# Gates and gated unit by seven block products ahead of one mixing stage for both halves

## The chip, the cores and the metric

The kernel runs on one core of a Trainium2 chip. Its time is the device time of one execution in microseconds (us), 2001.92 as the median of three runs (2001.01 to 2002.47). The engines that matter are TensorE (PE in the profile; PEld is its loading of weights), VectorE (DVE), ScalarE (ACT), GpSimd (POOL) and SyncE (SP, here a queue of transfers). Each engine works off its own queue of instructions in order and waits, where it must, for the results of another engine or of a transfer.

## The reference

One layer of a language model's trunk, on x of 1024 tokens by 1024 channels, in float32. Cut to what matters:

```python
h = layer_norm(x, ln_in_g, ln_in_b)
u = h @ w_in                    # columns: a, g | z | x, B, C | dt | gate_a | gate_b
v = a * sigmoid(g)                              # gated unit, 1024 channels
v = silu(layer_norm(causal_dwconv(v, 31 taps))) # norm over channels, for each token
y_a = v @ w_conv_out
xbc = silu(causal_dwconv([x, B, C], 4 taps))
dt = softplus(dt_raw + dt_bias)
y = ssd_chunked(x, dt, -exp(a_log), B, C) + x * d_skip   # 32 heads in 4 groups, chunks of 128
y = rms_norm_by_group(y * silu(z)) * norm_w
y_b = y @ w_ssm_out                             # 2048 -> 1024
h = layer_norm(alpha * h + (sigmoid(gate_a) * y_a + sigmoid(gate_b) * y_b) @ w_o)
up = causal_dwconv(h @ w_ffn_up, 3 taps)        # 2 x 2816 channels
h = layer_norm(alpha * h + (silu(up[:2816]) * up[2816:]) @ w_ffn_down)
```

The scan `ssd_chunked` carries a state from chunk to chunk, so chunk c + 1 of a group needs the state that chunk c leaves.

## The kernel before

Tokens are worked on in two halves of 512 (HALF), channels in blocks of 128 (the partitions). Every operand of a large product is split into a high part (fp32r) and the rest, and a product of two is three matmuls, hi by hi, hi by lo, lo by hi (`mm3`). A weight tile of 128 x 1024 is loaded by SP, its high part is made by ACT, and its low part by DVE (`weights`). `project` multiplies such a tile with a split activation of eight slices, 24 matmuls of 128x512.

The program runs `ln_in_first` (norm of the first half, transposed to `hT0`), `mixers(0)`, `combine(0)` with the norm of the second half inside it, `out_proj`, `mixers(1)`, `combine(1)`, and the feed-forward part.

- `mixers(hh, hT)`: `first_columns` (dt, B, C of group 0), `time_steps` (softplus of dt and its running sums, a long chain of small steps in the tile `sp`), and then for each of four groups: columns B, C and four of x with their 4-tap convolution (`conv4`), the gate z, two channel blocks of the gated unit (`glu`, a weight for a and one for g), the scan of the group (`ssd_group`, four chunks), and the 31-tap convolution of the two blocks (`conv31`, on DVE, 30 instructions SCALAR_TENSOR_TENSOR for each block, "taps" below), at a low priority. At the end come the eight column blocks of gate_a.
- `combine(hh)`: the eight blocks of gate_b in turn with the second half of `w_ssm_out` (weights `sp`), the norm of the convolution over channels (the pieces `cc` come back from DRAM; POOL adds them up, TensorE averages over partitions with `mean_w`, DVE subtracts, ACT squares, POOL adds, and so on, until DVE and ACT write the split result `sT`), `w_conv_out` (weights `co`), and the split of the mixed result into `mixT`.
- The feed-forward up-projection already works with all 1024 tokens at once and with seven block products in place of eight (a 2 x 2 block product by Winograd's form of Strassen's method): `up_first` makes two of the seven and stores them to DRAM, `up_rest` the other five.

The order of the instructions on each engine is set when the kernel is built, by a scheduler which takes them in the order in which they are written, shifted by the numbers in `tc.high_priority(offset=...)`: a positive offset pulls a piece ahead, a negative one leaves it until nothing else is there.

The names of the profile: `sm` and `acc` are banks of PSUM, `w_xx` a split weight, `st_xx` its raw form, `c` and `v` the convolution's result and input, `stats` and `csq` the norm's sums. Lines that the prediction uses: L166 to L168 the three matmuls, L154 and L155 the split of a weight, L435 the taps, L493 the product `au` (on POOL) of the scan, L294 to L351 the time steps, L638 to L658 the norm, L182 and L183 the split of `sT`.

## Time and profile before

| what | value |
|---|---|
| median of three runs | 2001.92 us |
| profiled execution, its own time | 2004.89 us |
| its span | 2003.2 us |
| granted TensorE clock, mean | 0.997 |
| TensorE, DVE, ACT, POOL busy | 98%, 84%, 52%, 9% |

The same by stage (from the engines' busy times in stretches of the span, us):

| stage | from, to | TensorE | DVE | ACT | POOL |
|---|---|---|---|---|---|
| norm, first half | 0 to 41 | 25.9 | 28.3 | 14.0 | 10.9 |
| mixers, first half | 41 to 530 | 486.6 | 449.2 | 280.7 | 40.4 |
| combine and out-projection | 530 to 700 | 170.0 | 121.9 | 69.2 | 26.4 |
| mixers, second half | 700 to 1190 | 488.9 | 450.9 | 274.7 | 39.1 |
| combine, second half | 1190 to 1330 | 138.6 | 88.6 | 66.9 | 20.9 |
| up-projection | 1330 to 1770 | 439.8 | 357.9 | 237.9 | 39.9 |
| down-projection, last norm | 1770 to 2003 | 217.0 | 194.9 | 90.9 | 3.3 |

How to read the rows: a timeline row is start, duration, engine, line, operation, written tile, read tiles, shape and count, and in brackets how long the engine had been idle and for whom. A group's row has the busy time and the mean duration in ns of one instruction, and then the idle time before them. A waits row has the total, the number and the longest. Instructions overlap in their engine's pipeline, so the step from one start to the next is often shorter than a duration. A row of stretches has, after the bounds, the busy time of PE, PEld, DVE, ACT and POOL, the granted clock, the DMA share and GB/s.

### The profile page before, as it was taken

What the parts mean: (1) busy time and instruction counts of PE and PEld (TensorE: products, weight loads), DVE (VectorE), ACT (ScalarE), POOL (GpSimd) and SP (SyncE); (2) the same over time, 40 slices, a digit from 0 to 9 for tenths busy, and PEclk for the clock granted to TensorE, in tenths of its full rate; (3) what the DMA queues carried; (4) which work ended last, traced back from release to release, by engine and by line L of the source; (5) the groups of instructions that cost most, each with busy time, mean ns of one, the idle gap of its engine ahead of it and who ended that gap; (6) DMA issues with size and microseconds to landing.
All of it is one profiled execution on the core that took longest, in us unless ns stands there. A gap on an engine that the chain in (4) does not pass through costs nothing.

```text
span 2003.2 us, 24740 instructions
## 1 busy us (share of the span) xinstructions
PE 1966.7 (98%) x9092; PEld 1618.2 (81%) x9092; DVE 1691.6 (84%) x2243; ACT 1034.2 (52%) x1491; POOL 180.8 (9%) x189
## 2 busy tenths in 40 slices
...
PEclk9999999999999999999999999999999999999999
...
GB/s 211 95 74 95 79 78 118 95 110 101 165 207 163 164 121 74 85 90 85 116 90 111 100 170 124 132 283 236 144 183 181 182 173 190 165 278 299 197 244 126
DMA packets 109449, 297.12 MB, mean 148 GB/s; under 512 B 12560, under 2 KB 12560, under 8 KB 109328
## 3 DMA queue, kind: packets, MB, share of 16 engines
...
q8 instruction: 71, 1.16, 0.2%
...
## 4 chain that ended last, share of the span: by engine, by line
PE 71%; DVE 21%; DMA 4%; issue 3%; ACT 1%; DVEq 0%; SPq 0%; ACTq 0%
PE acc L168 16%; PE acc L167 16%; PE acc L166 16%; DVE c L435 8%; PE sm L168 6%; PE sm L167 6%; PE sm L166 6%; DMA do<-wdown 2%; DVE xbc L390 2%; PE sm L549 1%; PE sm L192 1%; DMA b_scr<-fo 1%; PE sm L530 1%; PE acc L372 1%; DVE w_so L155 1%
## 5 line engine op out<-in xcount | busy, mean ns | idle before, releaser
L435 DVE SCALAR_TENSOR_TENSOR c<-v,pc,c 128x512 f32<-128x512 f32 x480 | 375.4, 805 | 7.3 <-ACT c L424 5.9
L493 POOL TENSOR_TENSOR au<-seg_mv,head_of 128x1024 fp32r<-128x1024 f32 x32 | 76.8, 2399 | 908.3 <-PE sm L502 727.0
L166 PE MATMUL acc<-hT,w_c 128*128 128x512 f32 x376 | 150.3, 400 | 0.0
L167 PE MATMUL acc<-hT,w_c 128*128 128x512 f32 x376 | 149.9, 399 | 0.0
L168 PE MATMUL acc<-hT,w_c 128*128 128x512 f32 x376 | 147.7, 393 | 0.0
L1016 ACT CAST w_dn<-dr 128x1024 fp32r<-128x1024 f32 (+1 forms) x73 | 68.6, 944 | 82.3 <-DVE dr L953 30.8
L390 DVE SCALAR_TENSOR_TENSOR xbc<-u,pc,xbc 128x512 f32<-128x512 f32 x144 | 109.9, 775 | 0.8 <-ACT xbc L388 0.8
L167 PE MATMUL sm<-h1s,w_s 128*128 128x512 f32 x264 | 102.7, 389 | 0.0
L166 PE MATMUL sm<-h1s,w_s 128*128 128x512 f32 x264 | 102.7, 389 | 0.0
L168 PE MATMUL sm<-h1s,w_s 128*128 128x512 f32 x264 | 102.2, 389 | 0.0
L154 ACT CAST w_c<-st_c 128x1024 fp32r<-128x1024 f32 x50 | 52.6, 1051 | 94.2 <-PE acc L168 76.5
L167 PE MATMUL acc<-w_z,hT 128*128 128x512 f32 x256 | 100.9, 394 | 0.0
L166 PE MATMUL acc<-w_z,hT 128*128 128x512 f32 x256 | 100.8, 401 | 0.0
L168 PE MATMUL acc<-w_z,hT 128*128 128x512 f32 x256 | 100.4, 395 | 0.0
L167 PEld LDWEIGHTS acc<-hT,w_c 128*128 128x128 f32 x376 | 70.6, 188 | 17.8 <-issue 3.9
L168 PEld LDWEIGHTS acc<-hT,w_c 128*128 128x128 f32 x376 | 70.6, 188 | 17.0 <-issue 2.6
L166 PEld LDWEIGHTS acc<-hT,w_c 128*128 128x128 f32 x376 | 70.6, 188 | 16.9 <-issue 2.6
L1017 DVE TENSOR_TENSOR w_dn<-dr,w_dn 128x1024 fp32r<-128x1024 f32 (+1 forms) x73 | 78.5, 1087 | 3.2 <-ACT w_dn L1016 3.2
L155 DVE TENSOR_TENSOR w_c<-st_c,w_c 128x1024 fp32r<-128x1024 f32 x47 | 60.5, 1288 | 22.7 <-ACT w_c L154 22.7
L168 PE MATMUL acc<-h1b,w_ue 128*128 128x512 f32 x176 | 68.7, 394 | 0.0
L166 PE MATMUL acc<-h1b,w_ue 128*128 128x512 f32 x176 | 68.7, 390 | 0.0
L167 PE MATMUL acc<-h1b,w_ue 128*128 128x512 f32 x176 | 68.5, 389 | 0.0
...
## 6 DMA issues: line engine op xcount, KB each, us to landing
...
```

What stands on the lines that cost most here:

```text
L154: A.copy(w[:, 0, :], st)
L155: (eng or V).tensor_tensor(out=w[:, 1, :], in0=st, in1=w[:, 0, :].bitcast(F32), op=ALU.subtract)
L166: TE.matmul(ps, wa(0), xa(0), start=start, stop=False, skip_group_check=more)
L167: TE.matmul(ps, wa(0), xa(1), start=False, stop=False, skip_group_check=more)
L168: TE.matmul(ps, wa(1), xa(0), start=False, stop=stop, skip_group_check=more)
L192: TE.transpose(pt[:, i * P : (i + 1) * P], src[:, (q + i) * P : (q + i + 1) * P], ident)
L372: TE.matmul(ps[:, ts], w[:, i, k * P : (k + 1) * P], hT[:, j, k, ts], start=n == 0 and k == 0, stop=n == 2 and k == KD - 1,)
L390: V.scalar_tensor_tensor(out=o, in0=u[:, k : k + HALF], scalar=pc[:, wc + k : wc + k + 1], in1=o, op0=ALU.mult, op1=ALU.add,)
L435: V.scalar_tensor_tensor(out=accs[i], in0=v[:, k : k + HALF], scalar=pc[:, wc + k : wc + k + 1], in1=accs[i], op0=ALU.mult, op1=ALU.add,)
L493: G.tensor_tensor(out=au, in0=seg_mv[:, c, :].unsqueeze(1).to_broadcast([P, 8, P]), in1=head_of[:, g, :].unsqueeze(2).to_broadcast([P, 8, P]),
L1016: A.copy(w[:, 0, cs], src)
L1017: V.tensor_tensor(out=w[:, 1, cs], in0=src, in1=w[:, 0, cs].bitcast(F32), op=ALU.subtract)
```

## The change

The gates and the gated unit (the 32 column blocks of a, g, gate_a, gate_b) are computed for all 1024 tokens in a stage of their own, the front, as 16 pairs of blocks: `pair_first` makes two of seven block products (three pairs at half width, while the norm still runs), `pair_rest` the other five. The norm of all eight row tiles and the block sums of h stand ahead of it (`front_blocks`). The gated unit goes to DRAM as `v_scr`, the gates as `g_scr`, and the transposed second half as `h2_scr`; `second_half` reads that back and splits it into `hT1`.

The 31-tap convolution of channel blocks 0 to 2 is made in the front over all tokens (128x1024); the others are put into one `mixers` stage for both halves by the table `CONVS`, and three into the stage behind it. There is one buffer for its input and one for its result, and they are loaded and stored by POOL's queue.

In `mixers` a group's scan is now written ahead of the next group's columns, `au` is made by ACT (eight instructions in place of one on POOL), and PSUM is seeded by ACT copies in place of some DVE additions. Both halves' `ssm_out_second` end their half's scan, and only behind the second one come the convolution's norm of the first half (`conv_norm(0)`), its projection, the norm of the second half, `out_proj(0)` and the second projection. In the down-projection one stream of loads goes from SP's to POOL's queue, and 75 dummy transpositions stand at the very start (`warm`).

```diff
+CONVS = {n: ((3 + n, 0),) for n in range(5)} | {
+    5: ((3, HALF),),
+    6: ((4, HALF),),
+    7: (),
+}
...
+    def front_blocks(tp, qp, cv):
...
+        firsts_by_halves(tp, qp, b1, range(3))
+        sums = [qp.tile([P, 2, 4, HALF], F32R, name=f"hs{i}") for i in (1, 2, 3)]
+        b2 = big_tile("hb2")
+        for t in range(4):
+            with tc.high_priority(offset=1500):
+                xt = row_tile(4 + t)
+                norm(4 + t, xt)
...
+                G.dma_start(h2_scr[:, :, ts], st)
...
+                parts(lambda i: sums[0][:, i, :, ts], b22)
+                add(t0, b12, b22, ALU.subtract)
+                add(t2, t0, raw[:, 0:4, ts], ALU.subtract)
...
+    def second_half(pl):
+        hT = big_tile("hT1")
+        for k in range(KD):
+            r = pl.tile([P, HALF + 3], F32, tag="u", bufs=3, name=f"hr{k}")
+            G.dma_start(r[:, :HALF], h2_scr[:, k, :])
+            split_to(hT, k, r[:, :HALF])
...
+    def conv31(cv, segs, taps, behind):
...
+            if t0:
+                G.dma_start(vs, v_scr[i][:, t0 - H : t0 + n])
...
+        for k in range(H):
+            for vs, cs, i, t0, n, wc in todo:
+                ins = V.scalar_tensor_tensor(
...
+        for vs, cs, i, t0, n, wc in todo:
+            for t in range(t0, t0 + n, HALF):
+                G.dma_start(c_scr[t // HALF][i], cs[:, t - t0 : t - t0 + HALF])
...
-            G.tensor_tensor(
-                out=au,
-                in0=seg_mv[:, c, :].unsqueeze(1).to_broadcast([P, 8, P]),
-                in1=head_of[:, g, :].unsqueeze(2).to_broadcast([P, 8, P]),
-                op=ALU.mult,
-            )
...
+            for h in range(8):
+                A.activation(
+                    out=au[:, h, :],
+                    in_=seg_mv[:, c, :],
+                    func=AF.Identity,
+                    scale=head_of[:, g, h : h + 1],
+                )
...
+    def ssm_out_second(pl, hh, yT):
...
+            project(ps, weights(wssm[j, 1], f"sp{hh}_{j}"), yT)
+            V.tensor_add(y, y, ps)
+            V.tensor_mul(y, y, gb)
+            G.dma_start(m_scr[hh][j], y)
+
+    def mixers(cv, hT, taps, convs):
...
+            with tc.high_priority(offset=1500):
+                time_steps(pl, 0, ps)
+            for n in range(8):
+                hh, g = divmod(n, 4)
...
+                done = ssd_group(pl, hh, g, xT, bT, cT, cols[1], ssq)
+                for i, t0 in convs[n]:
+                    conv31_later(cv, ((i, t0, HALF),), taps, True)
...
+                if g < 3:
+                    cols = columns(pl, hh, hT, g + 1)
+                else:
+                    ssm_out_first(pl, hh, yTs[0])
+                if n == 3:
+                    with tc.high_priority(offset=2000):
+                        hT = second_half(pl)
+                    ps = column(1, hT, CT_DT)
+                    cols = columns(pl, 1, hT, 0)
...
+                if g == 3:
+                    ssm_out_second(pl, hh, yTs[1])
+                if n == 3:
+                    with tc.high_priority(offset=1500):
+                        time_steps(pl, 1, ps)
...
+    def conv_norm(pl, hh):
...
+            G.dma_start(pair[:, i % 2, :], c_scr[hh][i])
...
+    warm(75)
...
+    pairs(open_front, qp, bl, "f", wfront, front_scr, NP, 12, 3, 3, front_rest)
...
+    mixers(cv, hT, taps, CONVS)
+    state_stack.close()
+    with pool("comb") as pl:
+        with tc.high_priority(offset=1500):
+            sT = conv_norm(pl, 0)
+        for i in (5, 6, 7):
+            conv31_later(cv, ((i, HALF, HALF),), taps)
+        mixT = conv_out(pl, 0, sT)
+        sT = conv_norm(pl, 1)
         rs = [pl.tile([P, D], F32, name=f"r0_{t}") for t in range(4)]
         out_proj(pl, rs, 0, mixT)
...
+        mixT = conv_out(pl, 1, sT)
```

The next listings show the order in which the engines' instructions stand. First TensorE around the convolution's norm of the first half, before (`w_sp` and `w_gb` are weights of the products between which the two averages with `mean_w` stand):

```order
L167 MATMUL acc_4437<-yT_2_3063,w_sp_2_4440 128x512
L642 MATMUL sm_4794<-stats_4785,mean_w 128x512
L168 MATMUL acc_4437<-yT_2_3063,w_sp_2_4440 128x512
...
L168 MATMUL acc_4537<-hT_198,w_gb_5_4540 128x512
L653 MATMUL sm_4819<-stats_4785,mean_w 128x512
L166 MATMUL acc_4537<-hT_198,w_gb_5_4540 128x512
```

And now, at the end of `ssm_out_second` of the second half:

```order
L175 MATMUL acc_9417<-yT_2_8598,w_sp_7_9420 128x512
L782 MATMUL sm_9476<-mean_9467,mean_w 128x512
L792 MATMUL sm_9501<-var_9468,mean_w 128x512
L173 MATMUL acc_9645<-sT_9505,w_co_0_9648 128x512
L173 MATMUL acc_9679<-sT_9505,w_co_1_9682 128x512
```

The two averages and the first use of `sT` stand next to each other, right behind the last product of the scan's output. POOL's queue at that place, before (`au` is the scan's product, L638 to L651 are the norm's sums):

```order
L493 TENSOR_TENSOR au_3_3_3825<-seg_mv,head_of 128x1024
L638 TENSOR_TENSOR stats_4785<-cc_0_4773 128x512
L640 TENSOR_TENSOR stats_4785<-stats_4785,cc_2_4776 128x512 x2
L640 TENSOR_TENSOR stats_4785<-stats_4785,cc_4_4779 128x512 x2
L651 TENSOR_TENSOR stats_4785<-stats_4785,csq_4786 128x512 x7
L203 DMA in_1_5148<-prow 128x1024
```

and now (`m_scr` takes the scan's gated output `yb`, `c` is the result of the convolution of block 6 and `v` the input of block 7):

```order
L714 DMA m_scr_194<-yb_7_9415 128x512
L773 DMA cc_0_9455<-c_scr_164 128x512 x2
...
L773 DMA cc_4_9958<-c_scr_165 128x512 x2
L400 DMA v_512_9608<-v_scr_175 128x542
L427 DMA c_scr_165<-c_512_9574 128x512
L778 TENSOR_TENSOR mean_9467<-cc_0_9455 128x512
L780 TENSOR_TENSOR mean_9467<-mean_9467,cc_2_9458 128x512 x2
```

The sums now stand behind the stores of `yb` and of a convolution's result. TensorE around the time steps of the first half, before (`w_z` are the weights of the gate z):

```order
L372 MATMUL acc_335<-hT_198,w_c_36_330 128x256 x20
L282 MATMUL sm_485<-ident,dtc_483 128x32 x4
L166 MATMUL acc_563<-hT_198,w_c_16_566 128x512
...
L167 MATMUL acc_723<-w_z_0_1_758,hT_198 128x512
L324 MATMUL sm_522<-upper,sp_ax_517 128x128 x4
L351 MATMUL sm_537<-sp_490,upper 128x128
L166 MATMUL acc_726<-w_z_0_0_729,hT_198 128x512
```

and now:

```order
L175 MATMUL acc_3171<-w_z_0_3_3261,hT_282 128x512
L441 MATMUL acc_3299<-ident,dtc_3297 128x32 x4
L510 MATMUL acc_3345<-sp_3304,upper 128x128
L510 MATMUL acc_3345<-sp_3304,later 128x128
L510 MATMUL acc_3345<-sp_3304,ones 128x128
L173 MATMUL acc_3609<-hT_282,w_c_17_3612 128x512
```

Between the transpositions of `dtc` and the first use of `sp` stood 117 rows of TensorE before, and now none. The last place is TensorE in the second half's last scan, between its chunks 1 and 2, before (`w_gt` are weights of gate_a, `xsd` and `m` operands that DVE makes for each chunk):

```order
L538 MATMUL sm_8890<-xsd_3_1_8880,bt_3_1_8882 128x512
L167 MATMUL acc_9135<-hT_5145,w_gt_1_9138 128x512
...
L549 MATMUL sm_8894<-xs_3_1_8876,m_3_1_8865 128x64 x8
L487 MATMUL sm_8907<-ident,xbc_12_8417 128x128
...
L168 MATMUL acc_9168<-hT_5145,w_gt_2_9171 128x512
...
L538 MATMUL sm_8942<-xsd_3_2_8932,bt_3_2_8934 128x512
```

and now:

```order
L658 MATMUL sm_8732<-xsd_3_1_8724,bt_3_0_8648 128x512
L160 MATMUL sm_8749<-ident,xbc_12_8345 128x128
...
L619 MATMUL sm_8773<-au_3_2_8763,seg_st 128x512
L668 MATMUL sm_8736<-xs_3_1_8720,m_3_1_8711 128x64 x8
L619 MATMUL sm_8777<-au_3_2_8763,seg_st 128x512
L643 MATMUL sm_8788<-state_2887,xbc_23_8306 128x512
L658 MATMUL sm_8793<-xsd_3_2_8785,bt_3_2_8761 128x512
```

Of the 68 rows that stood between the two `xsd` products most were products of gate_a; now 12 rows stand there, all of the scan itself. DVE's queue holds taps of the 31-tap convolution between the chunks' steps in both kernels, of channel blocks 6 and 7 before, of 4 and 5 now.

738 lines of the change are left out of this document (416 added, 322 removed).

## The prediction

> **What bounds the kernel now.** I read the page's head first, then the chain that ended last, then TensorE's waits.
>
> ```profile
> span 2003.2 us, 24740 instructions
> PE 1966.7 (98%) x9092; PEld 1618.2 (81%) x9092; DVE 1691.6 (84%) x2243; ACT 1034.2 (52%) x1491; POOL 180.8 (9%) x189
> PEclk9999999999999999999999999999999999999999
> PE 71%; DVE 21%; DMA 4%; issue 3%; ACT 1%; DVEq 0%; SPq 0%; ACTq 0%
> ...
> PE sm L192 <- DVE x L230: 14.3, 2, 12.7
> PE acc L167 <- DVE w_dn L1017: 3.5, 3, 1.7
> ...
> PE acc L167 <- DVE yT L199: 1.4, 1, 1.4
> ```
>
> TensorE is busy for 98% of the span at full granted clock. Its waits, after 14.3 us at the start, are a few microseconds in all. So TensorE's own work sets the time, and DVE (84%) is close behind it. A removed matmul shortens the kernel only as long as every other engine still keeps ahead; a place where TensorE's queue holds nothing else to do turns another engine's whole duration into time. I therefore price two things: the work TensorE loses, and each place in the new order where it has no filler.
>
> **The gain.** The 32 column blocks of gates and gated unit took 8 block products per pair and now take 7: 32 x 8 slices x 3 matmuls x 2 halves / 8 = 192 matmuls of 128x512 fewer (7864 to 7672 in the order; the other matmul shapes stay but for 4 transpositions and 75 dummy ones in the start's idle). What is one worth?
>
> ```profile
> 599.78 0.39 PE L168 MATMUL acc<-sT,w_co 128*128 128x512 f32 x1
> ...
> 601.37 0.39 PE L166 MATMUL acc<-sT,w_co 128*128 128x512 f32 x1
> ```
>
> A row says 0.39, but the matmuls overlap: these are the first and the last of eight in a row, seven steps in 1.59 us, 0.227 each. 192 x 0.227 = -43.6 us. Taking 0.39 would give -74.9 and be wrong by the overlap.
>
> **The start, +4 (1 to 9).** TensorE's steady stream begins at 41.15, when it has done about 21 us of work (32 transpositions, 144 half-width matmuls), so the start costs about 20.
>
> ```profile
> 4.64 1.29 DVE L207 BATCH_NORM_STATS2 st_in<-x 128x6 f32<-128x512 f32 x2 [2.04 <-DMA x<-x]
> 8.79 2.48 DVE L227 SCALAR_TENSOR_TENSOR x<-x,mv_in,in_g 128x1024 f32<-128x1024 f32 x2 [1.22 <-DMA in_g<-prow]
> 31.49 9.37 PE L372 MATMUL acc<-hT,w_c 128*128 128x256 f32 x74
> 41.15 0.50 PE L166 MATMUL acc<-hT,w_c 128*128 128x512 f32 x1
> ```
>
> In the new order DVE must also norm rows 4 to 7 and form block sums before the stream runs. Its instructions up to the split of w_fe4 add up to 41.7 us; from 4.64, and with the same 1.22 us for in_g, that ends at 47.5. TensorE has 23 us of work until then, so the start costs 24. The low end is a cover by what I count as serial, the high end the second rows' loads, which wait behind stores on POOL's queue.
>
> **The front, +8 (4 to 10).** DVE prices, start to start:
>
> ```profile
> 599.43 1.28 DVE L227 SCALAR_TENSOR_TENSOR x<-x,mv_in,in 128x1024 f32<-128x1024 f32 x1
> 600.62 1.22 DVE L155 TENSOR_TENSOR w_co<-st_co,w_co 128x1024 fp32r<-128x1024 f32 x1
> 601.76 0.16 DVE L223 RECIPROCAL rs_in<-rs_in 128x1 f32<-128x1 f32 x1
> ...
> 603.02 0.68 DVE L626 TENSOR_TENSOR mb<-mb,gb 128x512 f32<-128x512 f32 x1
> 603.62 0.68 DVE L673 TENSOR_TENSOR gl<-gl,acc 128x512 f32<-128x512 f32 x1
> 117.29 1.40 DVE L435 SCALAR_TENSOR_TENSOR c<-v,pc,c 128x512 f32<-128x512 f32 x2
> 106.06 3.11 DVE L435 SCALAR_TENSOR_TENSOR c<-v,pc,c 128x512 f32<-128x512 f32 x4
> ```
>
> So 1.19 for a tap of 1024 tokens, 1.14 for a two-input operation of 1024, 0.60 of 512, 0.70 for a tap of 512, 0.78 where each waits for the last one. While pair 10 of the front is worked off, DVE has 20 taps (23.8), 10 operations of 1024 (11.4) and 23 of 512 (13.8), 49.0 us, between a value that TensorE gives and the split of w_fe14 that it needs; TensorE has 193 matmuls there, 43.8. That is 5.2. Up to w_fe15 the same count gives 7.1 + 3.4 + 6.0 = 16.5 against 13.7, 2.8 more.
>
> **Rebuilding the second half, +2 (0 to 4).** Eight slices come from h2_scr, each split by ACT and DVE (0.60), beside the first columns that read them.
>
> **Time steps, +16 (10 to 20).** Before, the softplus chain ran beside projections. Now TensorE's queue has the transpositions of dtc, then the three small matmuls that need the finished sp, with nothing between, once for each half.
>
> ```profile
> 43.46 1.28 ACT L296 ACT_TABLE_LOAD   x1
> ...
> L295 ACT ACTIVATE sp<-sp x1: 320/320/320, 43.0 to 43.0; 128x128 f32<-128x128 f32 x1
> L296 ACT ACTIVATE sp<-sp x1: 338/338/338, 44.8 to 44.8; 128x160 f32<-128x160 f32 x1
> L298 DVE RECIPROCAL sp<-sp x1: 947/947/947, 45.9 to 45.9; 128x128 f32<-128x128 f32 x1
> L305 DVE TENSOR_TENSOR sp<-sp x6: 284/289/293, 50.9 to 57.2; 128x128 f32<-128x128 f32 x6
> ```
>
> One chain: 0.32 + 1.28 + 0.34 on ACT, 0.95 for the reciprocal, sixteen small DVE steps, at up to 0.29 each some 4.4, and the four transpositions with the handing over between engines, 0.6: about 8. Twice: 16. ACT and DVE may have parts done ahead (low end); two additions of the output stand in the second chain (high end).
>
> **The last group's SSD, +26 (20 to 36).** In the second half's group 3 the gate columns that stood between the chunks are gone from TensorE's queue, while DVE's still holds taps there, now of channel blocks 4 and 5. Between t of group 2 and the last slice of yT, DVE has 55 taps (38.5), 8 scalings (5.6), 34 operations of 512 (20.4), 8 of 1024 (9.1) and 1.0 of small ones: 74.6. TensorE has 132 matmuls (30.0) and the chunks' smaller ones, 18.4 by the spacing of their like: 48.4. Both ends are tied by data, so the difference of 26 is TensorE's wait. The high end takes dependent taps at 0.78 and the round trips of each chunk.
>
> **The convolution's norm, +50 (38 to 58).** Before, the same chain ran under other projections:
>
> ```profile
> 528.44 1.30 POOL L638 TENSOR_TENSOR stats<-cc 128x512 f32<-128x512 f32 x1 [47.58 <-DMA cc<-c_scr]
> 529.86 10.28 POOL L640 TENSOR_TENSOR stats<-stats,cc 128x512 f32<-128x512 f32 x6
> 544.01 4.87 DVE L645 TENSOR_TENSOR cc<-cc,sm 128x512 f32<-128x512 f32 x8 [1.73 <-PE sm L642]
> 546.04 11.59 POOL L651 TENSOR_TENSOR stats<-stats,csq 128x512 f32<-128x512 f32 x7 [5.90 <-ACT csq L650]
> 562.16 3.35 DVE L655 RECIPROCAL stats<-stats 128x512 f32<-128x512 f32 x1 [2.44 <-ACT stats L654]
> 566.51 4.89 DVE L658 TENSOR_TENSOR cc<-cc,stats 128x512 f32<-128x512 f32 x8
> 571.91 0.68 DVE L183 TENSOR_TENSOR sT<-cc,sT 128x512 fp32r<-128x512 f32 x1
> ...
> L166 PE MATMUL acc<-sT,w_co x128: 389/389/389, 595.9 to 1298.9; 128*128 128x512 f32 x128
> ```
>
> From POOL's first addition to the first finished slice of sT it took 43.5 us, and TensorE asked for it only at 595.9. (That last row's time is the first use.) Now the queue of TensorE reads w_sp1_7, mean, var, w_co0_0. POOL's first addition stands behind the store of yb1_7, which needs w_sp1_7's product, and behind the store of c6, whose last eight taps (6.3 at 0.78) follow on DVE. Two additions (1.2), those taps and two issues make about 9, then 43.5, less the 1 us of the two matmuls: some 51 until sT arrives; the slices behind it come faster than three interleaved blocks use them. I take 50. Low end: POOL's 14 additions at 1.3 (its first row) in place of 1.7, and no c6 tail. High end: the c7 taps between.
>
> **The second norm, +7 (0 to 10).** It lies under w_co0, but eight subtractions of cc1 (4.9 as above) and some 2.9 of other rows stand on DVE before the split of w_wo0_0_0, which TensorE needs 0.5 us later.
>
> **The clock, +5 (2 to 10).**
>
> ```profile
> 26.54 1.72 PE L192 MATMUL sm<-ident,x 128*128 128x128 f32 x8 [1.60 <-DVE x L230]
> ...
> 27.00:28.00 1.00, 1.00 (x7) 1.00 (x6) 0.59 (x1) 0.56 (x1) 0.00 (x0) 0.50 0.78 319
> ...
> 29.00:30.00 1.00, 1.00 (x7) 1.00 (x7) 0.61 (x1) 0.00 (x0) 0.00 (x0) 0.50 1.16 262
> 30.00:31.00 1.00, 1.00 (x9) 1.00 (x9) 0.00 (x0) 0.00 (x0) 0.00 (x0) 0.90 0.69 258
> ```
>
> Behind a wait of 1.60 the granted clock (third number from the right) was 0.50 for some 3.3 us, a loss of 1.7. The two time steps and the norm make three such holes outside stretches that DVE paces: 5. The Trainium skill, "TensorE: Matmul & The Clock Gate", Part 1, says that an idle window of about 3.4 us halves the clock and as long a busy one restores it; by that the subtractions' hole of 7 would count as a fourth and the sum would be 1.7 higher, while this row shows a drop behind a shorter wait.
>
> **What goes, -3 (0 to -5).** The small waits of the mixing stages, of which the 1.4 above is one. GpSimd loses 32 products of 128x1024 to ACT (8 ACTIVATE each, ACT is at 52%), which costs TensorE nothing where it isn't waiting.
>
> **Sum.** -43.6 + 4 + 8 + 2 + 16 + 26 + 50 + 7 + 5 - 3 = +71.4. The profiled execution took 2004.9 (span 2003.2), 3.0 above the median of 2001.9; so 2001.9 + 71.4 = 2073. All low ends together give 2028, all high ends 2115.
>
> **Rivals.** *The norm is hidden anyway (8%).* If POOL came to the eight sums before w_sp1_7 ended, the 50 and its clock would go: 2073 - 52 = 2021. For it: the first half's c is in DRAM long before. Against: POOL's order, where the additions stand behind a store that needs w_sp1_7.
>
> *GpSimd's relief pays (6%), faster.* The chain gives DVE 21%, and DVE stretches beside GpSimd:
>
> ```profile
> L493 POOL TENSOR_TENSOR au<-seg_mv,head_of 128x1024 fp32r<-128x1024 f32 x32 | 76.8, 2399 | 908.3 <-PE sm L502 727.0
> 173.10 3.05 DVE L435 SCALAR_TENSOR_TENSOR c<-v,pc,c 128x512 f32<-128x512 f32 x2
> ```
>
> These two taps ran beside one such product, at 1.5 in place of 0.70. Were TensorE paced by that in the mixers, all 76.8 could come back: 2073 - 77 = 1996. It decides from 71 of the 77 on. Against it: TensorE waits next to nowhere in the mixers.
>
> *The norm is dearer (14%).* If the nine c7 taps that stand before the reciprocal run at 1.5 and POOL's 14 additions stretch alike, from 1.7 to 2.3, it is +7 and +9: 2089. The subtractions, with one operand in PSUM, took 0.61 each beside nothing and are no witness. The Trainium skill, "SBUF — State Buffer", "Who interferes with whom", says that a DVE instruction with two SBUF inputs and a GpSimd one that reads SBUF block each other for a whole instruction; by that each tap could wait out an addition, and the estimate would be 13 x 1.7 = 22, 2095.
>
> *The waits eat just the gain (2%):* 2002.
>
> **Chances and range.** The forecast itself has 70%. From 2018 to 2108 takes in the hidden norm and the dearer one, and leaves out the faster and the equal one and the ends where nearly all bounds fall on one side, together less than 2 in 10. A change under 0.2% can't be told from none here: faster 6%, same 2%, slower 92%.
>
> **What would show it.** TensorE's waits: mean_w's first matmul (L782) some 50 us behind w_sp1_7; two holes of about 8 at L510; waits of some 26 in all on DVE between so1_4 and sp1_0; w_fe14 and w_wo0_0_0 late by 5 and 7. The count of matmuls would be right and the busy time of TensorE down by about 43 in spacing, whatever the end. I am wrong if POOL's additions start before w_sp1_7 ends, if the taps run far below 0.70, or if a wait that I count twice is one: a late TensorE gives DVE time to catch up.

## The result, and the profile after

The changed kernel takes 2156.39 us (median of 4 runs, 2151.48 to 2157.73) where the kernel before took 2002.2 beside it: 1.0759 times as long, interval 1.0746 to 1.0772. The forecast was 2073, range 2018 to 2108. The sign was right and the price half of what it is: +71 forecast, +154 measured, and the time lies outside the range.

The profiled execution took 2151.48, the fastest of the four, so the traces are compared by their spans: 2149.8 against 2003.2, +146.6. So the traces account for 146.6 of the 154; the difference of two medians can part by some 6 us from that of two traces, and nothing below 6 is read out of either.

The page of the changed kernel: its head, the clock, the chain that ended last.

```profile
span 2149.8 us, 25077 instructions
PE 1972.1 (92%) x8979; PEld 1606.9 (75%) x8979; DVE 1700.7 (79%) x2197; ACT 1143.9 (53%) x1839; POOL 169.8 (8%) x300
PEclk9999999999999998999998858999999999999999
PE 57%; issue 21%; DVE 10%; DMA 7%; ACT 5%; POOL 1%; SPq 0%; DVEq 0%; POOLq 0%; ACTq 0%
```

TensorE fell from 98% to 92% of a longer span, no other engine filled up, and the clock has a dent just past the middle (8, 8, 5, 8) and a single 8 at the second time steps, where before every digit was 9. Nothing bounds this kernel throughout. Here is what TensorE waits for:

```profile
PE sm L782 <- POOL mean L780: 35.3, 1, 35.3
PE acc L510 <- DVE sp L469: 22.6, 2, 13.9
PE acc L173 <- ACT sT L189: 16.3, 1, 16.3
PE sm L792 <- POOL var L790: 15.3, 1, 15.3
PE sm L668 <- ACT sm L665: 11.1, 4, 7.1
PE acc L173 <- ACT w_wo L148: 8.6, 1, 8.6
PE acc L173 <- ACT zs L559: 6.5, 4, 3.7
PE sm L173 <- ACT ffuv L1021: 5.5, 5, 2.9
```

Three single waits of 35.3, 15.3 and 16.3 are the norm. The two of L510 are the time steps, and the 8.6 lies at the second norm. The rest are many small ones, most of which end on ScalarE.

To put a price on each place I use the **lag**: the time at which a matmul starts in the trace, less the work that stands ahead of it in TensorE's queue, each matmul counted at the spacing of its like (0.227 us for 512 columns at full clock). Where TensorE goes ahead undisturbed the lag all but stays; each wait, and each stretch at half clock behind a wait, adds to it. At the end the lag is 256.8 in the changed kernel and 66.8 before: +190. The work itself is 43.0 lower. 190 - 43 = 147, the difference of the spans. (Some 8 us of dummy matmuls, which fill TensorE's waiting at the changed kernel's start, count as no work.)

Not all of a lag is waiting. Matmuls that follow each other at full clock lie a little wider than counted, above all in the scan: this adds 33 us in the changed kernel and 32 before, while before the lag stands still under plain projections (it moves by 0.1 from 596 to 687). So the third column has the waits and the stretches at half clock alone, added up from the start times. (Numbers in us, by the lag at the first matmul of w_fs3_0, w_c0_0, w_c0_4, w_sp0_7, w_c1_17, w_so1_0, w_sp1_3, w_co0_3 and w_ue0.)

| stretch | lag gained | of it waits and half clock | forecast, its share of the clock's 5 included |
|---|---|---|---|
| work | | -43.0 | -43.6 |
| start | 23.2 (before 20.9) | +2.3 (difference of the lags) | +4 |
| front | 22.1 | +18.7 | +8 |
| time steps, both | 11.7 + 17.9 | +28.4 | +19.3 |
| mixers otherwise | 25.1 + 19.5 | +21.2 | -1 (rebuilding 2, what goes -3) |
| last group | 39.7 | +35.2 | +26 |
| norm | 75.4 | +75.4 | +51.7 |
| second norm, to the up-projection | 12.1 | +11.4 | +7 |
| up- and down-projection | 10.0 (before 10.6) | -0.6 (difference of the lags) | 0 |
| waits before, from the start to the up-projection | | -6.0 | |
| wider spacing there, 29.8 against 26.5 | | +3.3 | |
| sum | | +146.3 | +71.4 |

The sum agrees with the 146.6. Most of the error lies in the norm (24 too low), the mixers (22), the front (11), and the last group and the time steps (9 each). Across these rows goes the clock: matmuls that follow each other at half clock lost 28.9 us here and 3.0 before, so 26 where 5 were forecast.

### The profile page after: what moved, and what is told of

Read it like the earlier page. It is cut to its first block, busy times and chain, and to the rows that moved or that the text cites. A ratio compares the mean times of both kernels' runs of the same rounds, so it can differ in the third digit from the quotient of the medians.

```text
span 2149.8 us, 25077 instructions
## 1 busy us (share of the span) xinstructions
PE 1972.1 (92%) x8979; PEld 1606.9 (75%) x8979; DVE 1700.7 (79%) x2197; ACT 1143.9 (53%) x1839; POOL 169.8 (8%) x300
## 3 DMA queue, kind: packets, MB, share of 16 engines
q1 hardware_dynamic: 88848, 240.49, 33.7%
## 4 chain that ended last, share of the span: by engine, by line
PE 57%; issue 21%; DVE 10%; DMA 7%; ACT 5%; POOL 1%; SPq 0%; DVEq 0%; POOLq 0%; ACTq 0%
PE acc L173 11%; PE acc L175 11%; PE acc L174 11%; PE sm L175 7%; PE sm L173 7%; PE sm L174 7%; DVE c L415 4%; PE sm L160 1%; DMA dr<-wdown 1%; PE sm L668 1%; DVE w_fs L906 1%; DMA gb<-g_scr 1%; ACT au L610 1%; DMA frb<-wfront 1%; PE acc L362 1%
## 5 line engine op out<-in xcount | busy, mean ns | idle before, releaser
L415 DVE SCALAR_TENSOR_TENSOR c<-v,pc,c 128x512 f32<-128x512 f32 (+1 forms) x390 | 347.7, 891 | 34.6 <-ACT c L406 29.7
L173 PE MATMUL acc<-hT,w_c 128*128 128x512 f32 x400 | 158.8, 399 | 2.4 <-ACT zs L559 2.4
L174 PE MATMUL acc<-hT,w_c 128*128 128x512 f32 x400 | 159.7, 399 | 0.6 <-DVE hT L190 0.6
L175 PE MATMUL acc<-hT,w_c 128*128 128x512 f32 x400 | 159.8, 400 | 0.0
L175 PE MATMUL acc<-w_z,hT 128*128 128x512 f32 x256 | 103.9, 408 | 0.0
L173 PE MATMUL acc<-w_z,hT 128*128 128x512 f32 x256 | 103.0, 404 | 0.6 <-ACT xbc L527 0.6
L174 PE MATMUL sm<-h1s,w_us 128*128 128x512 f32 x264 | 102.7, 389 | 0.0
L173 PE MATMUL sm<-h1s,w_us 128*128 128x512 f32 x264 | 102.7, 389 | 0.0
L175 PE MATMUL sm<-h1s,w_us 128*128 128x512 f32 x264 | 102.2, 389 | 0.0
L174 PE MATMUL acc<-w_z,hT 128*128 128x512 f32 x256 | 101.5, 397 | 0.0
L173 PEld LDWEIGHTS acc<-hT,w_c 128*128 128x128 f32 x400 | 76.2, 190 | 21.6 <-ACT zs L559 3.9
L175 PEld LDWEIGHTS acc<-hT,w_c 128*128 128x128 f32 x400 | 75.9, 190 | 18.2 <-issue 2.6
L174 PEld LDWEIGHTS acc<-hT,w_c 128*128 128x128 f32 x400 | 76.0, 190 | 17.9 <-issue 1.7
L173 PE MATMUL sm<-hs,w_fs 128*128 128x512 f32 x192 | 76.2, 399 | 9.3 <-ACT ffuv L1021 5.5
L610 ACT ACTIVATE au<-seg_mv,head_of 128x128 fp32r<-128x128 f32 x256 | 80.0, 398 | 3.4 <-DVE seg_mv L500 3.4
L175 PE MATMUL sm<-hs,w_fs 128*128 128x512 f32 x192 | 75.7, 396 | 2.9 <-DVE w_fs L906 2.8
L668 PEld LDWEIGHTS sm<-xs,m 128*128 128x128 f32 x512 | 63.5, 198 | 17.4 <-ACT sm L665 14.0
```

The lines of the kernel that those rows point to most:

```text
L173: TE.matmul(ps, wa(0), xa(0), start=start, stop=False, skip_group_check=more)
L174: TE.matmul(ps, wa(0), xa(1), start=False, stop=False, skip_group_check=more)
L175: TE.matmul(ps, wa(1), xa(0), start=False, stop=stop, skip_group_check=more)
L415: ins = V.scalar_tensor_tensor(out=cs, in0=vs[:, k : k + n], scalar=taps[:, wc + k : wc + k + 1], in1=cs, op0=ALU.mult, op1=ALU.add,)
L610: A.activation(out=au[:, h, :], in_=seg_mv[:, c, :], func=AF.Identity, scale=head_of[:, g, h : h + 1],)
L668: TE.matmul(py[:, hs], m[:, h, :], xs[:, hs], start=not seeded and h == 0, stop=True, skip_group_check=seeded or h > 0,)
```

## The experiments

All times are medians; "against after" means against 2156.4. The lag table stands behind the runs.

### The gain alone

`eight`: one of the seven block products of the front's pairs is made twice, 192 matmuls more.

```diff
+        if nm == "f":
+            product(ps, lambda i: w24[:, i, HALF:], bl["b22"], False)
         product(ps, lambda i: w24[:, i, HALF:], bl["b22"], False)
```

> In each of the 16 pairs one block product is done twice, which puts the 192 matmuls back (the doubled product makes the gates and the gated unit wrong). If TensorE paces the front, the time grows by their full 43.6 us, to 2200. If DVE and ACT pace it by what the lag says, about 20 us of them are covered: 2156 + 24 = 2180. Rival (a matmul is worth its row's 0.39): 2156 + 75 = 2231.

2193.6, +37.2 by the medians; the spans differ by 43.1 (2192.9 against 2149.8), and the lag at the end is the same within 0.5. So of the 43.6 for 192 matmuls all come back by the traces, and 37 by the medians (the changed kernel's trace is of its fastest execution): the gain was what was worked out, or at most some 6 less. What went wrong is in the prices of the waits and of the clock.

### The norm: where do 75 us come from?

GpSimd's timeline from the last store of yb to the first sum, in the changed kernel:

```profile
1233.45 0.54 POOL L714 DMA_DIRECT2D m_scr<-yb  x1 [4.35 <-DVE yb L713]
1233.98 1.09 POOL L773 DMA_DIRECT2D cc<-c_scr  x2
1236.80 4.32 POOL L773 DMA_DIRECT2D cc<-c_scr  x8 [1.73 <-issue]
1243.38 0.55 POOL L773 DMA_DIRECT2D cc<-c_scr  x1 [2.26 <-DMA cc<-c_scr]
...
1250.54 0.55 POOL L400 DMA_DIRECT2D v<-v_scr  x1 [1.04 <-DMA cc<-c_scr]
1251.75 0.54 POOL L427 DMA_DIRECT2D c_scr<-c  x1 [0.66 <-DMA cc<-c_scr]
1252.31 1.27 POOL L778 TENSOR_TENSOR mean<-cc 128x512 f32<-128x512 f32 x1
```

I had counted one store, the taps of c6, two additions and two issues ahead of the first sum: 9 us. In the queue stand fourteen loads of cc too, those of the second half's norm among them, at 0.54 each to issue, and from the eleventh on each issue waits until an earlier load has landed. From the yb store's issue to the first sum it is 18.9 us. VectorE then had its own trouble:

```profile
1263.28 5.13 DVE L415 SCALAR_TENSOR_TENSOR c<-v,pc,c 128x512 f32<-128x512 f32 x5 [23.95 <-ACT c L406]
1268.33 4.86 DVE L784 TENSOR_TENSOR cc<-cc,sm 128x512 f32<-128x512 f32 x8
1273.11 1.81 DVE L415 SCALAR_TENSOR_TENSOR c<-v,pc,c 128x512 f32<-128x512 f32 x1
1274.85 2.28 DVE L149 TENSOR_TENSOR w_co<-st_co,w_co 128x1024 fp32r<-128x1024 f32 x1
...
1293.92 3.34 DVE L794 RECIPROCAL var<-var 128x512 f32<-128x512 f32 x1
```

It stood idle for 24 us, since c7's taps need the v that is loaded behind those fourteen; five of them then ran ahead of the subtractions; and ahead of the reciprocal stand nine more and three splits of w_co, which took 20.8 us beside GpSimd's additions, where they would take some 9.7 at 0.70 and 1.14. Three runs take these apart.

`loads_sp`: the loads go to SyncE's queue.

```diff
-            G.dma_start(pair[:, i % 2, :], c_scr[hh][i])
+            SY.dma_start(pair[:, i % 2, :], c_scr[hh][i])
```

> Edit: the loads of the convolution's channels for the norm (cc<-c_scr) are issued on SyncE's queue and no longer on GpSimd's. Theory A: in the changed kernel GpSimd's first addition came 23 us behind w_sp1_7, where 9 were forecast, because GpSimd issued fourteen loads and a store one after the other ahead of it; on another queue these 14 us of the norm go: about 2143. Theory B: the loads are late because the DMA engines are full just then, or the chain is bound by VectorE's taps behind it: within 4 of 2156.

2136.7, -19.7, and the norm's lag falls from 75.4 to 59.2. GpSimd's first sum now starts with the store:

```profile
1233.77 0.54 POOL L714 DMA_DIRECT2D m_scr<-yb  x1 [4.34 <-DMA cc<-c_scr]
1234.46 1.58 POOL L778 TENSOR_TENSOR mean<-cc 128x512 f32<-128x512 f32 x1
1241.07 0.57 POOL L400 DMA_DIRECT2D v<-v_scr  x1 [5.03 <-issue]
```

Theory A holds: 16 us of the norm were the queue. (The time fell by 6 more than its 2143.)

`tail_noconv`: channels 4 to 7 of the second half without their convolution.

```diff
-    6: ((4, HALF),),
+    6: (),
...
-        for i in (5, 6, 7):
-            conv31_later(cv, ((i, HALF, HALF),), taps)
+        for i in (4, 5, 6, 7):
+            v = cv.tile([P, VW], F32, tag="v", name=f"vx{i}")
+            G.dma_start(v[:, :HALF], v_scr[i][:, HALF:])
+            G.dma_start(c_scr[1][i], v[:, :HALF])
```

> Edit: channels 4 to 7 of the second half's convolution are left out (v is copied to c_scr in place of c), so the 124 taps of 512 tokens that stand on VectorE behind group 2 of the mixers are gone; all else stays as in the changed kernel, so its output is not that of the reference. Theory A: the wait of TensorE in the last group (39 us by the trace) and the norm's excess over 50 (23 us) come from these taps, 124 x 0.70 = 87 us of VectorE: the first falls by some 25, the second by some 15 to 23, and the run takes about 2110. Theory B: these waits are the length of the chains themselves (ScalarE's decay products, GpSimd's sums and the loads on its queue), and VectorE's taps only fill holes: 2140 or more.

2118.5, -37.9, nearer to A's 2110. The norm falls to 58.1 (theory A's 15 to 23), the second norm from 11.8 to 0.3. But the last group falls only from 39.7 to 33.7, where A said 25: there it is B so far. I come back to it.

`norm_bare`: both edits.

> Edit: the two edits of tail_noconv and loads_sp together: channels 4 to 7 of the second half's convolution left out, and the norm's loads on SyncE's queue. Theory A: taps and loads are two separate parts of the norm's wait; they add up, 2156 - 38 - 20 = 2098, and from the end of w_sp1_7 to the first product of w_co0 only the bare chain is left, 40 to 46 us. Theory B: both edits take the same delay away (the channel's load and store that stand ahead of the norm's loads on GpSimd's queue): 2110 or more.

2111.1, -45.3, so the sum of the two edits (-57.6) is not reached: by the total it is B. The norm itself falls to 47.0 of lag, or 41.5 from the end of w_sp1_7 to the first product of w_co0, as A had it: 75.4 is 47 of bare chain, 16 of queue and 17 of taps, less 5 that both take away. These 5 are a part of what the total misses; the rest isn't located. GpSimd's additions show the bare chain:

```profile
1236.04 1.27 POOL L778 TENSOR_TENSOR mean<-cc 128x512 f32<-128x512 f32 x1
...
1257.66 1.26 POOL L790 TENSOR_TENSOR var<-var,mean 128x512 f32<-128x512 f32 x1
1259.00 1.27 POOL L778 TENSOR_TENSOR mean<-cc 128x512 f32<-128x512 f32 x1
```

### Giving the norm a cover

`sp_woven`: the products of the second half's w_sp1 stand between the norm's steps in TensorE's queue.

```diff
-                if g == 3:
+                if n == 3:
                     ssm_out_second(pl, hh, yTs[1])
...
+        norm = conv_norm(pl, 0)
         with tc.high_priority(offset=1500):
-            sT = conv_norm(pl, 0)
+            next(norm)
+        ssm_out_second(pl, 1, yT, range(3), 2)
+        next(norm)
+        ssm_out_second(pl, 1, yT, range(3, 6), 2)
+        sT = next(norm)
+        ssm_out_second(pl, 1, yT, range(6, 8), 2)
```

> The second half's eight products w_sp1 are moved behind the start of the first half's convolution norm and woven between its steps; nothing is left out. Theory A (TensorE's queue held nothing beside the norm): of the 73 us that TensorE falls back between w_sp1_4 and w_co0_0 the 43.5 us of products cover 35 to 43, so about 2156 - 40 = 2116 us. Rival B (POOL's queue, DVE and the transfers are overloaded there, and filler only shifts the wait): less than 20 us are won, 2136 or more. A ninth of the chain, the loads of cc ahead of the first addition, should shrink under A as well, since they no longer stand behind the stores of yb1.

2138.8, -17.6: B. Last group and norm together fall from 115.1 to 79.7, so 35 are covered; but the second norm grows from 11.8 to 32.4.

`norm_early`: mean and variance are made while groups 2 and 3 run.

```diff
+    def norm_stats(pl):
...
+                G.tensor_add(mean, mean, c)
+                A.activation(out=c, in_=c, func=AF.Square)
+                G.tensor_add(var, var, c)
...
+            TE.matmul(pm, mean_w, t, start=True, stop=True)
...
+        SY.dma_start(n_scr, nst)
...
+                if n == 6:
+                    norm_stats(pl)
...
-            sT = conv_norm(pl, 0)
+            sT = norm_apply(pl, 0)
```

> Edit: the mean and the variance of the first half's convolution (eight loads, GpSimd's sums, the two mean_w products, the square root and the reciprocal; the variance as mean of squares less square of the mean) are worked out while the second half's groups 2 and 3 run, and kept in DRAM; behind the mixers only loads, one subtraction, one product, the activation and the splits of each channel stand ahead of w_co0. Theory A: the 73 us at the norm are its chain of sums with TensorE idle; what is left is the loads and one channel's steps, 12 to 25 us, and the run takes 2096 to 2108. Theory B: the sums cost the same again where they now run, since VectorE, ScalarE and GpSimd's loads there already make TensorE wait: 2125 or more.

2141.4, -15.0. A's statement on the place is right: the norm's lag falls from 75.4 to 32.0. Its time is wrong: the mixers' second half takes 8 of it back (27.2 for 19.5), the second norm 24 (35.5 for 11.8).

`early_au`: the same with the decay products on GpSimd and the second norm's loads on SyncE's queue.

> Edit: norm_early, with the decay products au back on GpSimd and the second norm's loads on SyncE's queue. Theory A: the parts are independent and add up: some 13 for au and 5 or more for the second norm below norm_early. Theory B: GpSimd's products of 2.4 us each and its sums stand in each other's way, or VectorE's taps stretch beside both: no less than norm_early by 5.

2135.5, 5.9 below norm_early instead of 18. The mixers gained (52.1 to 35.2 in both halves together), the last group lost 12. The outcome lies next to B, whose bound of 5 it passes by 1; that GpSimd's products and sums hinder each other isn't shown by it.

Why does the second norm take it back? In sp_woven, and in `all_woven` below, GpSimd's last store of c and what follows stand here (all_woven's timeline):

```profile
1328.19 0.57 POOL L427 DMA_DIRECT2D c_scr<-c  x1 [23.32 <-issue]
1333.46 1.25 POOL L785 TENSOR_TENSOR mean<-mean,cc 128x512 f32<-128x512 f32 x1 [4.70 <-DMA cc<-c_scr]
```

The channel c7 of the second half is done at 1328. In the changed kernel this store stood at 1325.01, in sp_woven at 1331.03; in every kernel that keeps these taps (eight apart) it lies between 1313 and 1337. The second norm's sum needs it, so a TensorE that comes to the second average early waits there for longer. The changed kernel's own second norm is another wait: GpSimd's last sum was done at 1334.6, TensorE came to the average at 1349.23 and went through, and then it stood for 8.6 until w_wo0 was cast. Its raw tile was issued at 1351.24, on SyncE's queue behind loads that wait for VectorE's mixing of the last block. Where the taps are gone (tail_noconv: 0.3) the second norm vanishes; but there the second average also runs at 1283, among the first products of w_co0, so that alone doesn't show which of the two did it.

### The front

`front_taps`: the first three channels' taps cut from 30 to 1.

```diff
-            conv31_later(cv, ((j, 0, T),), taps)
+            conv31_later(cv, ((j, 0, T),), taps, nk=1)
```

> Of the 30 taps of channel blocks 0 to 2 in the front only one is left, so DVE has about 104 us less in the front and the convolution of these channels is left out. Theory A (DVE with the taps between the splits sets the front's pace): of the 22 us that TensorE falls back in the front 15 to 20 go, 2156 - 17 = 2139 us. Rival B (ACT's copies and the reload of the first products from DRAM set it): 5 us or less, 2151 or more.

2156.7: no change, B. `front_noconv`: this convolution left out whole.

```diff
-            conv31_later(cv, ((j, 0, T),), taps)
+            for t in range(0, T, HALF):
+                G.dma_start(c_scr[t // HALF][j], a[:, t : t + HALF])
```

> Edit: in the front, the convolution of channels 0 to 2 is left out whole, its load of v and its taps (the gated unit is stored in place of c); the output is not that of the reference. Theory A: the front's 22 us of lag come from the convolution standing in ScalarE's and VectorE's order there, where ScalarE's first step of it waits for the load of v: some 15 us come back, 2141. Theory B: the lag is that of VectorE's and ScalarE's gates and block sums themselves: 2150 or more, with the front's lag still near 20. Theory C: the front's lag falls but is given back in the mixers, which VectorE and ScalarE pace: 2150 or more, with the lag at the mixers' end as before.

2147.0 by the median, but the lag of the front is 21.7 against 22.1 (29.6 in front_taps; kernels whose front is as in the changed one show 22 to 28): B on the front, though the time lies 3 below B's bound. The two kernels in the middle of it, changed and front_noconv (stretch, TensorE, PEld, VectorE, ScalarE, GpSimd, clock, share of DMA, GB/s):

```profile
165.00:195.00 30.00, 28.85 (x125) 22.94 (x124) 29.04 (x32) 12.59 (x17) 1.06 (x2) 1.00 0.43 140
```
```profile
165.00:195.00 30.00, 28.07 (x117) 22.69 (x116) 16.45 (x20) 12.18 (x17) 1.62 (x3) 0.94 0.46 149
```

VectorE went from 97% to 55% busy and TensorE won nothing. My count of VectorE's work against TensorE's was beside the point. What TensorE waits for there (front_noconv, 60 to 320) is ScalarE emptying the banks of its products:

```profile
PE sm L173 <- ACT ffug L1026: 6.5, 3, 2.7
PE sm L173 <- ACT ffuv L1021: 4.3, 4, 2.9
PE sm L173 <- ACT fs L1018: 1.6, 2, 1.0
```

`front_prio`: those copies ahead of the casts of weights on ScalarE.

```diff
-        A.copy(s, ps)
+        with tc.high_priority(offset=4000 if nm == "f" else 0):
+            A.copy(s, ps)
```
(and the same for the copies of uv and ug)

> Edit: in the front's pairs, the three copies with which ScalarE empties the banks of TensorE's products (s, uv, ug) get a priority above the casts of the next pairs' weights, so that on ScalarE ug's copy stands ahead of a cast of w_fs instead of behind it. Theory A: with VectorE's taps gone the front kept its lag, and TensorE's waits there end on these copies, which stand behind casts that wait for other things; the lag of 37 at the mixers' start falls by some 10 and the run takes about 2145. Theory B: the copies are late because the products before them have only the 2.7 us of another product to hide copy and VectorE's step, whatever the order: within 4 of 2156.

2143.4, -13.0, yet the front's lag is 21.0 for 22.1: on the place it is B. What fell is the second time step (14.2 for 17.9) and the mixers of the second half (11.7 for 19.5), of which the last group took back 4. I have no reason for that to show; the edit lets the scheduler place other things differently too. The copies end the waits in the front, but what makes them late isn't settled.

### Time steps

`steps_split`: the softplus chain ahead of the first columns in the program, its last matmuls behind them.

```diff
+            with tc.high_priority(offset=1500):
+                finish = time_steps(pl, 0, ps)
             cols = columns(pl, 0, hT, 0)
             ssq = sums_tile(pl, 0, 0)
-            with tc.high_priority(offset=1500):
-                time_steps(pl, 0, ps)
+            finish()
```
(and the same for the second half)

> The softplus chain of the time steps is written ahead of the first columns and its last matmuls behind them, for both halves; nothing is left out. Theory A (TensorE waits only because the matmuls on sp stand right behind the transpositions of dtc): the 12 and 19 us of these two places go down to 2 or less each, 2156 - 28 = 2128 us (2122 to 2136). Rival B (the chain is long because ACT and DVE are late there anyway): the wait moves to the first use of the columns, and less than 8 us are won, 2148 or more.

2156.4: B. The holes of L510 are gone, but the wait moved to the four transpositions at their head, which now have to wait for dtc: 31.6 + 1.1 in front and first step, where it was 22.1 + 11.7. In the second half the lag was 9 lower when the last group began, and that group cost 53.4 for 39.7.

Why was the second hole 13.9 and the first 8.7? VectorE's timeline in the changed kernel:

```profile
835.83 0.69 DVE L712 TENSOR_TENSOR yb<-yb,acc 128x512 f32<-128x512 f32 x1 [5.92 <-DMA yb<-y_scr]
840.74 0.95 DVE L458 RECIPROCAL sp<-sp 128x128 f32<-128x128 f32 x1
845.58 0.69 DVE L712 TENSOR_TENSOR yb<-yb,acc 128x512 f32<-128x512 f32 x1 [3.88 <-DMA yb<-y_scr]
850.50 0.29 DVE L469 SCALAR_TENSOR_TENSOR sp<-dtv,sp 128x128 f32<-128x128 f32 x1
```

I had counted two additions of the output inside the chain, 1.4 us. What counts is that VectorE takes its queue in order and stands for 5.92 and 3.88 before them, until yb is loaded, with the steps of sp behind. Of the 5.92 TensorE pays 2.7 ahead of the hole, as a wait of the transpositions (`PE acc L441 <- DVE yb L712: 2.7, 1, 2.7`); the 3.88 stand inside it. `gb_two` gives every other block's gate another buffer, so that the loads can go ahead.

```diff
+            odd = hh == 0 and j % 2
-            gb = pl.tile([P, HALF], F32, tag="gb", name=f"gb{hh}_{j}")
+            gb = pl.tile(
+                [P, HALF], F32, tag="xs" if odd else "gb", bufs=2 if odd else 1, name=f"gb{hh}_{j}"
+            )
```

> Edit: in the first half's second output projection, the gate's tile gb of every other block lies in a second buffer (one of xs, which is free there), so that the loads of gb and yb for the next block don't wait until VectorE has multiplied with the last gate. All else as in the changed kernel. Theory A: the second time-step hole is longer than the first (13.9 against 8.7) because VectorE stands in its queue before yb additions whose loads come late, with the softplus steps behind them; the hole falls to 9 to 10 and the lag after it by 4 or more. Theory B: the hole is that of the chain and stays between 13 and 15. Whether the gain reaches the end: 2151 if it is kept, 2156 if the last group takes it back.

2149.9, -6.5, and the hole is 13.6: B in the number, but the edit missed its aim, as VectorE still stands for 6.29 and 3.52 before the same additions. What makes the loads late stays open (yb's own buffers, given back by stores, were not touched).

### The mixers and the last group

`au_pool`: the decay products back on GpSimd, as before the change.

```diff
-            for h in range(8):
-                A.activation(
-                    out=au[:, h, :],
-                    in_=seg_mv[:, c, :],
-                    func=AF.Identity,
-                    scale=head_of[:, g, h : h + 1],
-                )
+            G.tensor_tensor(
+                out=au,
+                in0=seg_mv[:, c, :].unsqueeze(1).to_broadcast([P, 8, P]),
+                in1=head_of[:, g, :].unsqueeze(2).to_broadcast([P, 8, P]),
+                op=ALU.mult,
+            )
```

> Edit: the decay products au go back from ScalarE (8 ACTIVATE each) to GpSimd (one product of 128x1024), as before the change. Theory A: ScalarE, which is busy for 40 to 44 of 50 us in the mixers, now paces them, and waits of TensorE and VectorE on it there (m, sm, zs) make up the 8 us in the mixers and a part of the 39 in the last group: some 10 to 20 come back, 2136 to 2146. Theory B: the move relieved VectorE, whose taps run at 1.5 beside such a product in place of 0.70; taking it back stretches VectorE in the last group, where it paces, by 8 products x 2.4 = some 10 to 19, and in the mixers by less: 2166 to 2180. Theory C: neither paces: within 4 of 2156.

2142.8, -13.6: A. The first half's mixers in the changed kernel, in au_pool and before (columns as above):

```profile
440.00:715.00 275.00, 269.30 (x1300) 217.00 (x1298) 220.14 (x304) 216.87 (x426) 3.94 (x9) 0.99 0.26 88
```
```profile
440.00:715.00 275.00, 273.01 (x1341) 222.10 (x1340) 244.32 (x316) 195.34 (x320) 38.82 (x28) 1.00 0.29 93
```
```profile
440.00:715.00 275.00, 273.58 (x1260) 224.90 (x1259) 218.34 (x291) 134.97 (x187) 35.02 (x27) 1.00 0.48 159
```

ScalarE was at 49% there before and stands at 79% now. The forecast had taken its 52% over the whole span and called the move free. With au back on GpSimd the mixers lose 34 instead of 45, although VectorE is then busier (244 against 220).

`mix_noconv`: the convolution of channels 3 to 7 left out for both halves.

```diff
                 for i, t0 in convs[n]:
-                    conv31_later(cv, ((i, t0, HALF),), taps, True)
+                    v = cv.tile([P, VW], F32, tag="v", name=f"vm{n}")
+                    G.dma_start(v[:, :HALF], v_scr[i][:, t0 : t0 + HALF])
+                    G.dma_start(c_scr[t0 // HALF][i], v[:, :HALF])
```
(and behind the mixers as in tail_noconv, for channels 5 to 7)

> Edit: the convolution of channels 3 to 7 is left out for both halves (v is copied to c_scr), so that none of its taps stands on VectorE in the mixers, the last group and the norm: 10 times 30 taps of 0.70, some 210 us of VectorE. Theory A: VectorE paces the mixers and the tail through these taps; the lag of TensorE before w_sp1_0 (125) falls by 20 or more beyond what channels 4 to 7 of the second half gave, and the run takes 2095 or less. Theory B: the waits in the mixers are the length of chains between TensorE, ScalarE and VectorE, and an idle VectorE doesn't shorten them: 2108 to 2122, as with the second half's channels alone.

2093.3, -63.1: A. Mixers 34.0 for 44.6, last group 18.6 for 39.7. The last group (1150 to 1200) in the changed kernel, in tail_noconv and in mix_noconv:

```profile
1150.00:1200.00 50.00, 34.49 (x148) 26.30 (x148) 46.74 (x70) 20.54 (x43) 1.86 (x4) 0.73 0.14 44
```
```profile
1150.00:1200.00 50.00, 39.44 (x181) 31.25 (x181) 26.04 (x38) 21.78 (x44) 0.54 (x1) 0.83 0.17 55
```
```profile
1150.00:1200.00 50.00, 42.96 (x188) 35.89 (x188) 22.63 (x32) 10.51 (x14) 3.78 (x7) 0.87 0.38 121
```

Two things make up the 39.7. About half (21) is the taps, but not those of channels 4 and 5 that I had counted there (6): the rest belongs to taps further ahead. In the kernels that keep these (eight apart, which is later by its added work), w_so1_4 starts between 1110 and 1131, whether TensorE came to w_so1_0 at 1047.5 or at 1084.7; without them it starts at 1099. The other half reads as a chain, which no run takes apart. This is tail_noconv's, with VectorE half idle (start, duration, what):

```profile
1168.98 1.15 DVE m L640
1170.26 1.98 PE sm L668 x16
1172.27 1.09 ACT m L627 x2
1173.35 0.52 ACT m L628
...
1175.12 1.22 DVE m L640
1176.33 0.61 DVE t L648
1176.97 0.60 ACT sm L665
1177.61 3.69 PE sm L668 x16
```

TensorE, ScalarE and VectorE hand one chunk to each other, and where no columns stand between, each step's whole duration is time. The sixteen small products cost 1.98 and then 3.69, at half clock behind the holes.

VectorE had time for its taps earlier, and didn't use it. The changed kernel and the one before, in the second half's mixers:

```profile
900.00:950.00 50.00, 48.52 (x244) 39.46 (x243) 33.07 (x44) 37.11 (x71) 0.00 (x0) 1.00 0.22 71
```
```profile
900.00:950.00 50.00, 50.00 (x248) 41.41 (x247) 50.00 (x68) 28.76 (x42) 4.28 (x2) 1.00 0.25 81
```

### Are the holes separate?

`steps_tail`: steps_split and tail_noconv.

> Edit: steps_split and tail_noconv together (softplus chain ahead of the columns, its last matmuls behind them; channels 4 to 7 of the second half's convolution left out). With steps_split alone the lag was 7 to 9 lower up to w_so1_0 and 4 higher at w_sp1_0. Theory A: it was VectorE's taps in the last group that took the gain back; without them it stays, some 8 below tail_noconv: 2110. Theory B: the last group has a floor that the taps don't set: within 4 of tail_noconv, 2115 to 2122.

2123.9, not below tail_noconv but 5 above: A fails, and B's range is missed by 2. The last group costs 39.0 in place of tail_noconv's 33.7, so the last four channels' taps are not what takes the gain back there.

`all_woven`: sp_woven, steps_split, loads_sp, au_pool and front_prio; `all_early` has norm_early in place of sp_woven; `all_gb` is all_woven with gb_two.

> Edit: sp_woven, steps_split, loads_sp, au_pool and front_prio in one kernel. Alone they gave -17.6, 0, -19.7, -13.6 and -13.0. Theory A: the holes are separate and the gains add up: about 2092. Theory B: a TensorE that comes earlier to the next place waits there for the same chain, so a good part is given back: 2105 to 2130.

> Edit: norm_early, steps_split, loads_sp, au_pool and front_prio in one kernel. Theory A: the gains add up: 2141 - 20 (loads, second norm) - 13.6 - 13 is below 2100. Theory B: given back as before, at the last group and at the second norm: 2115 to 2135.

> Edit: all_woven with the second gb buffer of gb_two. In all_woven the time steps' chain stood ahead of these blocks, so the loads matter only for how early TensorE comes to the last group, which has taken back such gains. Theory A (holes separate): 4 or more below all_woven, 2128 or less. Theory B (given back at the last group and the second norm): within 3 of all_woven, 2129 to 2135.

2132.0, 2144.1 and 2130.4: A fails each time. The first two lie 2 and 9 above B's ranges, so even more was given back than it had; the third is B. The gains of all_woven's five edits add up to 64; 24 are left. The lag by stretch (us):

| kernel | time | front | step 1 | mixers 1 | step 2 | mixers 2 | last group | norm | second norm |
|---|---|---|---|---|---|---|---|---|---|
| after | 2156.4 | 22.1 | 11.7 | 25.1 | 17.9 | 19.5 | 39.7 | 75.4 | 11.8 |
| front_noconv | 2147.0 | 21.7 | 12.2 | 25.1 | 17.8 | 22.7 | 38.0 | 71.6 | 11.1 |
| front_prio | 2143.4 | 21.0 | 12.0 | 27.5 | 14.2 | 11.7 | 43.5 | 74.8 | 10.6 |
| steps_split | 2156.4 | 31.6 | 1.1 | 35.4 | 7.5 | 13.2 | 53.4 | 71.7 | 11.7 |
| au_pool | 2142.8 | 25.3 | 11.4 | 16.9 | 17.7 | 17.3 | 44.1 | 71.7 | 10.4 |
| loads_sp | 2136.7 | 27.9 | 11.7 | 24.2 | 17.2 | 18.3 | 39.2 | 59.2 | 11.0 |
| tail_noconv | 2118.5 | 25.6 | 11.6 | 25.3 | 17.9 | 21.9 | 33.7 | 58.1 | 0.3 |
| norm_bare | 2111.1 | 27.4 | 11.8 | 26.1 | 17.9 | 21.6 | 33.5 | 47.0 | 0.3 |
| mix_noconv | 2093.3 | 25.6 | 12.7 | 16.8 | 16.5 | 17.2 | 18.6 | 58.2 | 0.3 |
| sp_woven | 2138.8 | 24.2 | 11.1 | 26.8 | 18.0 | 18.2 | 60.2 | 19.5 | 32.4 |
| norm_early | 2141.4 | 25.8 | 11.6 | 24.9 | 18.3 | 27.2 | 40.7 | 32.0 | 35.5 |
| all_woven | 2132.0 | 27.7 | 1.1 | 31.0 | 8.6 | 16.0 | 73.4 | 2.5 | 47.5 |

(In the rows with steps_split the time steps' wait lies at the end of front and of mixers 1; in those with sp_woven a part of the norm lies in the last group.) In all_woven the norm is hidden (2.5), and TensorE waits at the second norm instead:

```profile
PE sm L788 <- POOL mean L785: 38.0, 1, 38.0
PE sm L799 <- POOL var L796: 18.1, 1, 18.1
```

So the holes are not separate prices on one line. Two places, the last group and the second norm, take back most of what an edit gains ahead of them. At the second norm the rows show what sets the moment: VectorE's last taps, which GpSimd's sum needs. At the last group mix_noconv points at taps further ahead, but no run closes a hole with those gone, so there the cause is argued. No kernel of this study that computes everything beats the one before: the best, all_gb, takes 2130.4 (1.0649 times, 1.0631 to 1.0667).

## Why the prediction was wrong

Its direction was right, and nearly every place that it named as a hole is one. The gain came in as worked out (43.0 of 43.6; eight puts 37 to 43 of it back). Two terms failed most, the norm and "what goes". Term by term, with the third column of the table as measured:

- **The gain, the start, the up- and down-projection:** as forecast, within 2.
- **Front, +8; measured 18.7.** The forecast is less than half of it, and the reason wrong: "5.2" and "2.8" came from VectorE's work against TensorE's, and with that work nearly halved the front loses the same (front_taps, front_noconv). The waits end on ScalarE's copies out of PSUM.
- **Rebuilding, +2:** TensorE waits for the second half's hT for 0.6.
- **Time steps, +16 and 3.3 of the clock; measured 28.4.** The first is near (10.9, of which 8.7 are the hole). The second failed at "two additions of the output stand in the second chain (high end)": they take 1.4, while the rows show VectorE awaiting their loads, 2.7 of it ahead of the transpositions and 3.9 inside the hole. That this is the cause is argued from the rows; gb_two, which was to show it, didn't take the waits away.
- **"What goes, -3"; measured +21.2 in the mixers.** The step that failed is the sentence that au's move to ScalarE "costs TensorE nothing where it isn't waiting". It took ScalarE's 52% over the span for its share in this stage (79% now). au_pool puts 10.4 of it on au; mix_noconv finds 10.6 that go with the taps. Together that would be all of it, but both may be partly the same microseconds, and no run has both edits. That TensorE waited nowhere in the mixers before spoke of a queue with gate columns in it, and these were leaving.
- **Last group, +26; measured 35.2.** The sum of VectorE's work less TensorE's gave a number of the right order, but isn't what happens: of the lag of 39.7, 6 go with the taps counted there, 15 with taps further ahead, and 18.6 reads as the chain from chunk to chunk that only the high end took in.
- **Norm, +50; measured 75.4, 51.7 forecast with its clock.** The mechanism was right, and so was its base: the bare chain is 47.0. Mis-sized was "make about 9", which left out the fourteen loads and the waits for their landing on GpSimd's queue, 16 measured. And the rival "the norm is dearer" was no rival but a part: taps and splits ahead of the reciprocal at 2 to 2.5 times their length, which with c6 and c7 make 17. (The sign for it was put on the wrong row: "some 50 us behind w_sp1_7" is when sT was to come, not L782. L782 came 35.3 behind, the first use of sT 71.1.)
- **Second norm, +7; measured 11.4.** The place is right, the reason isn't: the eight subtractions ended at 1355.6, and VectorE then stood for 2.6 until w_wo0's raw tile had landed and was cast.
- **The clock, +5; 26 measured across the rows above.** Three holes were counted, and the half-clock stretches in the last group alone lost 10.6.

The price of a hidden norm was put at 52. norm_early hides 43 of it and gains 15: the sum treats each hole as a price of its own, and the runs show that a hole closed ahead of the last group or of the second norm opens there. All high bounds together gave 2115, which was still too low: "what goes" had no upper bound above zero, and the norm, the time steps, the front and the clock all passed theirs.
